# The output projection of a gated MLP as seven block products instead of eight, in a two-block transformer kernel on one NeuronCore

## Chip, core and metric

The kernel runs on one core of one Trainium2 chip, as one program. A time is the device time of one execution in microseconds (us); the time of a kernel is the median of its executions. A profile is of one execution, taken by the hardware profiler. The engines are named as the profile names them: PE (matrix multiply) with PEld (its weight loads), DVE (vector), ACT (scalar), POOL (GpSimd) and SP, which here only issues transfers (DMAs). All loads and stores that this text speaks of go through SP's one queue, in the order of the program.

## What is computed

Two layers over 1024 tokens of width 1024, batch 1, float32. The first block is a dilated attention beside a linear recurrence, whose outputs are merged; the second is a gated MLP, and then a sliding-window attention that shares k and v computed from the MLP's result. The change is in the MLP's last line:

```python
def gmlp_mixer(h, w_in, ln_g, ln_b, w_s, b_s, w_out):
    u, v, z = jnp.split(h @ w_in, 3, axis=-1)          # 3 x (1024 x 2048)
    u = jax.nn.gelu(u)
    v = layer_norm(jax.nn.gelu(v), ln_g, ln_b)
    ...                                                # s: a causal mix of v in chunks of 128 tokens
    y = u * s * jax.nn.silu(z)                         # 1024 x 2048
    return y @ w_out                                   # 2048 x 1024: the output projection

h = h + rms_norm_2(y, a_post_g[i])                     # y is the mixer's result here
kv_in = rms_norm_2(h, kv_norm_g)
k_shared, v_shared = kv_in @ w_k, kv_in @ w_v
```

## The kernel before

A float32 product is made of three matmuls of rounded halves (hi times hi, hi times lo, lo times hi), each of 128 rows by 512 columns over 128 inputs. So each operand tile of 128x512 is first split: ACT writes the hi part (`whi`, `y_hi`) and DVE subtracts it from the raw tile (`wlo`, `y_lo`). Matmuls write to banks of PSUM named `pb`, `pd` and `psP`; the same names serve many stages.

The order on every engine is the order in which the Python program issues instructions; nothing reorders them. The matmul loops call `tick()` every four matmuls. A tick counts down delayed stores (`store`, issued on SP some ticks after their data was requested), tries one step of weight loading and splitting (`w_step`: loads `L209`, splits `L285`/`L286`), and steps the lanes, which are Python generators whose `yield n` means "go on n ticks later". What lanes issue is thus laid beside the matmuls.

In order of time the parts that matter here are these. `phase1a` (to about 1150 us) is the dilated attention with its groups, merged per head pair in `lane_m` (POOL's `Og` and `Wb` lines); `phase2` (to 1337 us) the up-projections of both branches and the first output projection. `phase3` computes v (to 1553 us), then z and u in 16 passes of 128 columns each (to about 1870 us). A pass calls `seven`, which forms two 128x1024 results from seven products over half of the inputs instead of eight, with sums of the inputs made before, and differences of the weight blocks made by POOL (`L228`). Within a pass, c1, c5 and c2 are partial results; POOL adds u = c2 + c5 (`L421`) and c5 = c2 + c5 (`L424`), and DVE adds the PSUM banks (`L405`). Then `mixed` multiplies u, s and silu(z) to y (`L2207`, `L2211`, with POOL's `L2205`), and y goes to DRAM, tiles of 128x512 of the buffers Y for the two halves of the tokens.

The output projection is `out_proj("a_out", 16, ...)`, called `run(0)` and `run(1)` for the two halves of the tokens, from about 1874 us to 2057 us. Each half makes two column blocks of 512, for each of which it runs 16 k tiles by 4 token tiles by 3 matmuls: 192 matmuls (`L1843`), 768 in all. `stream` brings y back from DRAM (16 loads of 512 KB, `L1950`) and splits it (`L1710`, `L1711`). The result is read from PSUM by ACT (`Square` with a row sum, `L1850`) and by DVE (times the norm's gain, `L1851`). After a half, `norm` runs in `lane_n`: a chain of 11 small DVE instructions for the root mean square, the update of x (`xr`, `L1905`), ACT's squares (`L1910`), a second chain, the scaling (`L1923`), and then transposes on PE with copies by ACT and DVE (`L502`, `L503`), which are the operands `Ahi` and `Alo` of the next stage. That stage, from 2057 us on, forms v, k and q (`w_v`, `w_k`), again by halves of the tokens; its first two products for half 0 run while `norm` of the second half is still going on.

## Time and profile before

| what | value |
|---|---|
| time, median of 3 runs | 2487.09 us (2485.14 to 2487.64) |
| time of the profiled execution | 2485.88 us |
| its span, first to last instruction | 2484.1 us |
| mean granted clock of PE | 0.992 |
| PE busy | 2425.1 us, 98% |
| DVE / ACT / POOL busy | 56% / 41% / 29% |
| mean DMA traffic | 103 GB/s |
| z/u passes | 1553 to 1870 us |
| output projection | about 1874 to 2057 us |

The span is what the engines' instructions cover; the 1.8 us by which the execution is longer lie around it. The granted clock is the share of TensorE's full speed that the chip allowed.

### The profile page before, as it was taken

Reading aid. Unit: us, or ns where it says so; the run is one execution under the profiler, and the core shown is the slowest. Engines: PE = TensorE matmul, PEld = TensorE weight load, DVE = VectorE, ACT = ScalarE, POOL = GpSimd, SP = SyncE. Lnnn points to the kernel's source line nnn. Section 1 sums busy time; section 2 is a strip of 40 time slices with the busy share of each in tenths; the row PEclk is TensorE's granted clock in tenths of the full one; section 3 lists DMA queues with packets and bytes.
Section 4 is the critical chain, followed back from the end, with each engine's and each line's share of the span. In section 5 each row is a group of like instructions: output and inputs, shape, how many; then the busy total and the mean of one; then the engine's idle time right before and its main releaser. Section 6 shows DMA issues by size and latency. Waiting matters only on the chain.

```text
span 2484.1 us, 39818 instructions
## 1 busy us (share of the span) xinstructions
PE 2425.1 (98%) x14987; PEld 1917.3 (77%) x14987; DVE 1392.9 (56%) x3235; ACT 1021.4 (41%) x2515; POOL 714.7 (29%) x975
## 2 busy tenths in 40 slices
PE   8999999999999999999999999999999999999998
PEld 6788777777777777777788778888887887777777
DVE  6765345545454345566747347555556546556545
ACT  4433232223232256564244223444454434566632
POOL 3443044433544000222500244454450003201000
PEclk8999999999999999999999999999999999999999
DMA  5334321211122233466733232333335643100133
GB/s 145 102 107 132 69 68 42 58 43 52 48 56 68 80 93 118 128 212 195 238 143 139 86 110 85 102 102 88 95 102 208 217 131 108 41 19 26 32 117 132
DMA packets 271412, 256.94 MB, mean 103 GB/s; under 512 B 26251, under 2 KB 206539, under 8 KB 271220
## 3 DMA queue, kind: packets, MB, share of 16 engines
q1 hardware_dynamic: 271220, 254.40, 33.4%
q8 instruction: 118, 1.93, 0.3%
q14 instruction: 74, 0.61, 0.1%
HBM read 194.29 MB, written 60.06 MB: 102 GB/s over the span
## 4 chain that ended last, share of the span: by engine, by line
PE 83%; DVE 7%; ACT 4%; DMA 3%; issue 2%; SPq 0%; POOL 0%; DVEq 0%; ACTq 0%; POOLq 0%
PE pd L349 38%; PE pd L391 8%; PE psP L391 7%; PE pb L1843 7%; PE pd L1843 7%; PE psO L1157 2%; PE pb L1122 2%; PE pb L1056 2%; DVE wlo L286 1%; DMA vg<-Vd 1%; ACT P L1086 1%; PE pb L2193 1%; PE pb L349 1%; PE pb L743 1%; PE pb L925 1%
## 5 line engine op out<-in xcount | busy, mean ns | idle before, releaser
L349 PE MATMUL pd<-Ahi,wlo 128*128 128x512 f32 x1232 | 495.1, 402 | 4.0 <-DVE wlo L286 3.9
L349 PE MATMUL pd<-Ahi,whi 128*128 128x512 f32 x1232 | 496.2, 403 | 1.7 <-ACT whi L285 1.2
L349 PE MATMUL pd<-Alo,whi 128*128 128x512 f32 x1232 | 495.4, 402 | 0.3 <-DVE Alo L503 0.3
L286 DVE TENSOR_TENSOR wlo<-wraw,whi 128x512 fp32r<-128x512 f32 x356 | 267.4, 788 | 130.7 <-ACT whi L285 127.4
L349 PEld LDWEIGHTS pd<-Ahi,whi 128*128 128x128 f32 x1232 | 233.5, 190 | 54.4 <-issue 2.4
L349 PEld LDWEIGHTS pd<-Ahi,wlo 128*128 128x128 f32 x1232 | 233.4, 189 | 53.7 <-DVE wlo L286 5.4
L349 PEld LDWEIGHTS pd<-Alo,whi 128*128 128x128 f32 x1232 | 233.6, 190 | 52.8 <-issue 4.6
L285 ACT ACTIVATE whi<-wraw 128x512 fp32r<-128x512 f32 x356 | 203.3, 621 | 34.2 <-DMA wraw<-in_b_w_out_dram 12.4
L1711 DVE TENSOR_TENSOR wlo<-wraw,whi 128x512 fp32r<-128x512 f32 x144 | 121.0, 851 | 84.8 <-ACT whi L1710 84.8
L1086 ACT ACTIVATE P<-P,ST 128x192 f32<-128x192 f32 (+2 forms) x320 | 130.6, 409 | 57.6 <-DVE ST L1074 51.0
L1710 ACT ACTIVATE whi<-wraw 128x512 fp32r<-128x512 f32 x144 | 89.5, 623 | 91.4 <-POOL wraw L228 88.8
L349 PE MATMUL pd<-wlo,Ahi 128*128 128x512 f32 x256 | 101.6, 397 | 5.4 <-DVE wlo L286 5.4
L799 POOL TENSOR_TENSOR X<-UC,X 128x60 f32<-128x60 f32 (+24 forms) x248 | 78.1, 315 | 82.5 <-DVE UC L792 64.1
L349 PE MATMUL pd<-whi,Ahi 128*128 128x512 f32 x256 | 100.9, 394 | 0.1
L349 PE MATMUL pd<-whi,Alo 128*128 128x512 f32 x256 | 100.6, 393 | 0.0
L228 POOL TENSOR_TENSOR wraw<-wraw 128x512 f32<-128x512 f32 x48 | 63.0, 1313 | 98.7 <-DVE wlo L1711 90.1
L801 POOL TENSOR_TENSOR X<-X 128x60 f32<-128x60 f32 (+24 forms) x248 | 79.6, 321 | 19.4
L1157 PEld LDWEIGHTS psO<-PT,V 128*64 128x64 f32 x1040 | 55.5, 137 | 35.7 <-issue 17.7
L1157 PE MATMUL psO<-PT,V 128*64 128x128 f32 x1040 | 76.1, 283 | 6.0 <-DVE PT L1138 3.6
L278 POOL TENSOR_TENSOR wraw<-wraw,bpg 128x512 f32<-128x512 f32 x32 | 35.0, 1123 | 154.9 <-DMA wraw<-in_b_w_in_dram 142.9
L1122 PE MATMUL pb<-K,P 128*128 128x128 f32 (+1 forms) x388 | 62.5, 289 | 14.1 <-DVE P L1106 14.1
L1588 ACT ACTIVATE far<-pd 128x512 f32<-128x512 f32 x36 | 33.0, 918 | 101.9 <-PE pd L349 88.5
(434 smaller groups left out, 5398.7 us busy)
## 6 DMA issues: line engine op xcount, KB each, us to landing
wraw<-in_w_in_dram SPq DMA_DIRECT2D x82, 512.0 KB
wraw<-in_a_w_in_dram SPq DMA_DIRECT2D x48, 512.0 KB
wraw<-in_a_w_out_dram SPq DMA_DIRECT2D x32, 512.0 KB
QD<-far SPq DMA_DIRECT2D x36, 256.0 KB
gate<-GT SPq DMA_DIRECT2D x32, 256.0 KB
wraw<-in_w_out_dram SPq DMA_DIRECT2D x16, 512.0 KB
X<-xr SPq DMA_DIRECT2D x16, 512.0 KB
Vd<-v SPq DMA_DIRECT2D x32, 256.0 KB
```

Of the source, the lines that this page charges most:

```text
L285: nc.scalar.activation(out=his[j], in_=t[:, s], func=AF.Copy)
L286: nc.vector.tensor_tensor(out=los[j], in0=t[:, s], in1=his[j].bitcast(F32), op=ALU.subtract)
L349: nc.tensor.matmul(ps, lhsT=a, rhs=b, start=(n == 0), stop=(n == last))
L391: nc.tensor.matmul(ps, lhsT=a, rhs=b, start=(n == 0), stop=(n == 11))
L799: nc.gpsimd.tensor_tensor(out=tv, in0=U[:, j:j + 1, 0:j].to_broadcast([128, w, j]), in1=X[:, b0:8, j:j + 1].to_broadcast([128, w, j]), op= ...
L801: nc.gpsimd.tensor_tensor(out=X[:, b0:8, 0:j], in0=X[:, b0:8, 0:j], in1=tv, op=ALU.add)
L1086: nc.scalar.activation(out=it["P"][j][:, c], in_=Sx[j][:, c], func=AF.Exp, scale=-1.0, bias=ST[:, 0, n:n + 1], accum_out=ST[:, 1, n:n + 1])
L1122: tr = lambda x, m=128: nc.tensor.transpose(ps[0:m, 128 * x:128 * x + 128], Pt[:, 128 * x:128 * x + m], self.ident)
L1157: nc.tensor.matmul(O(h).rearrange("p (s x) -> p s x", s=2), lhsT=V[:, b - 1 + t, c:c + 64], rhs=rhs, start=t == tiles[0], stop=t == 1)
L1710: nc.scalar.activation(out=hi, in_=src, func=AF.Copy)
L1711: nc.vector.tensor_tensor(out=lo, in0=src, in1=hi.bitcast(F32), op=ALU.subtract)
L1843: nc.tensor.matmul(ps[j], lhsT=a, rhs=b, start=(k == 0 and n == 0), stop=(k == KT - 1 and n == 2))
```

## The change

With the inputs of the projection split in two halves of 1024 (A11, A12 for the first half of the tokens, A21, A22 for the second) and its weights in four blocks B11 to B22, the four result blocks are made from seven products of blocks, as `seven` does it for z and u: S1 = A21 + A22, S2 = S1 - A11, S3 = A11 - A21, S4 = A12 - S2 on the left, T1 = B12 - B11, T2 = B22 - T1, T3 = B22 - B12, T4 = B21 - T2 on the right, with the products A11 B11, S1 T1, S2 T2, A12 B21, S4 B22, S3 T3 and A22 T4 in this order.

Three places change. The z/u passes run in the order 0, 8, 1, 9, ..., so that both column halves of y are at hand, and a new lane (`sums`) makes the S tiles on POOL: one subtraction in a pass with a column tile under 8, three operations in the other, 32 of 128x512 in all; 56 tiles of 256 KB go to DRAM (`Y7`) in place of 32. Beside the dilated attention a new lane (`out_weights`) loads the four weight blocks tile by tile (32 loads of 256 KB), makes the T tiles on POOL (32 of 128x512) and stores them (32 stores of 256 KB, `TW`). And `out_proj` returns `run7` for `a_out`: seven products of 8 k tiles by 4 token tiles by 3 matmuls, 96 each, with the partial results joined by ACT, DVE and POOL; `norm(0)` starts behind product 4, `norm(1)` behind product 6.

```diff
-        by_half = lambda name, n: [dt(f"{name}{h}", [n, 128, 512]) for h in range(2)]
-        self.Y = by_half("Y", 16)
+        self.Y7 = [dt(f"Y7_{n}", [8, 128, 512]) for n in range(7)]
+        self.TW = [dt(f"TW{n}", [8, 128, 512]) for n in range(4)]
...
+        self.order_z = [8 * h + c for c in range(8) for h in range(2)]
+        fm("a_zu", a_in, [c for ct in self.order_z for c in (4096 + 128 * ct, 128 * ct)], kind="s")
+        self.first["a_out"] = len(pc)
+        v = km(I["a_w_out_2"][0])
+        T_ = lambda n: self.TW[n].rearrange("k p f -> p k f")
+        for b in (v[:, 0:8, 0:512], T_(0), T_(1), v[:, 8:16, 0:512], v[:, 8:16, 512:1024], T_(2), T_(3)):
+            for k in range(0, 8, 2):
+                pc.append((b[:, k:k + 2, :], "k", None))
...
+    def out_weights(self):
+        nc = self.nc
+        W = self.I["a_w_out_2"][0]
+        def load(r, c, k):
+            t = self.s2("tw")
+            nc.sync.dma_start(t, W[1024 * r + 128 * k:1024 * r + 128 * k + 128, 512 * c:512 * c + 512])
+            return t
+        def minus(x, y, to, n, k):
+            nc.gpsimd.tensor_tensor(out=to, in0=x, in1=y, op=ALU.subtract)
+            if n is not None:
+                self.store(self.TW[n][k], to, 4)
+        for k in range(8):
+            b11, b12, b22 = load(0, 0, k), load(0, 1, k), load(1, 1, k)
+            yield 10
+            minus(b12, b11, b11, 0, k)
+            yield 2
+            minus(b22, b12, b12, 2, k)
+            b21 = load(1, 0, k)
+            yield 2
+            minus(b22, b11, b22, 1, k)
+            yield 6
+            minus(b21, b22, b21, 3, k)
+            yield 5
     def phase1a(self):
         self.att_setup()
...
+        def run7(lanes, sums):
+            self.lanes = lanes + [sums]
+            self.w_lim = 12
+            og, x = ({}, {}), ({}, {})
...
+            def out(c, half, j, t, eng):
+                jk = self.s2("junk")
+                nc.scalar.activation(out=jk, in_=t, func=AF.Square, accum_out=ss[half][:, c, j:j + 1])
+                eng.tensor_tensor(out=t, in0=t, in1=gpost[:, 512 * c:512 * c + 512], op=ALU.mult)
+                og[half][c, j] = t
+            def plus(ps, t, to):
+                nc.vector.tensor_tensor(out=to, in0=ps, in1=t, op=add)
+                return to
+            def evac(n, j, ps):
+                if n < 2:
+                    t = (c1, c5)[n][j] = self.s2("og")
+                    nc.scalar.copy(out=t, in_=ps)
+                elif n == 2:
+                    c2[j] = plus(ps, c1[j], self.s2("og"))
+                elif n == 3:
+                    out(0, 0, j, plus(ps, c1[j], c1[j]), nc.gpsimd)
+                    u[j] = self.s2("og")
+                    nc.gpsimd.tensor_tensor(out=u[j], in0=c2[j], in1=c5[j], op=add)
+                elif n == 4:
+                    out(1, 0, j, plus(ps, u[j], u[j]), nc.vector)
+                elif n == 5:
+                    plus(ps, c2[j], c2[j])
+                    nc.gpsimd.tensor_tensor(out=c5[j], in0=c2[j], in1=c5[j], op=add)
+                    out(1, 1, j, c5[j], nc.gpsimd)
+                else:
+                    out(0, 1, j, plus(ps, c2[j], c2[j]), nc.vector)
+            i0 = self.first[name]
+            for n in range(7):
+                ps = [self.bank() for _ in range(3)] + [self.pd.tile([128, 512], F32, tag="pd", name="pd")]
+                if n == 1:
+                    self.drain(sums)
+                    self.flush()
+                    self.lanes = lanes
+                self.jit_limit = 4 * n + 8 if n else 6
+                if n in (4, 6):
+                    load_x(n // 6)
+                for kp in range(4):
+                    w = self.w_get(i0 + 4 * n + kp)
+                    for j in range(4):
+                        for k in (2 * kp, 2 * kp + 1):
+                            ah, al = [t[:, 128 * j:128 * j + 128] for t in act(k, n)]
+                            wh, wl = w(k % 2)
+                            for m, (a, b) in enumerate(((ah, wh), (ah, wl), (al, wh))):
+                                nc.tensor.matmul(ps[j], lhsT=a, rhs=b, start=(k == 0 and m == 0), stop=(k == 7 and m == 2))
+                        if kp == 3:
+                            evac(n, j, ps[j])
+                    self.w_free(i0 + 4 * n + kp)
+                if n == 4:
+                    self.lane_n.add(norm(0, og[0], x[0], ss[0], 18, 2))
+            self.drain(self.lane_n)
+            self.w_lim = 1000
+            self.lane_n.add(norm(1, og[1], x[1], ss[1]))
+            self.act_f, self.act_t = self.act_views(Ahi, Alo)
+            self.act_tiles = Ahi, Alo
...
+        return run7 if name == "a_out" else run
...
+        def sums(ct):
+            c = ct % 8
+            def do(x, y, op, n, to=None):
+                t = self.s2("ysum") if to is None else to
+                nc.gpsimd.tensor_tensor(out=t, in0=x, in1=y, op=op)
+                self.store(self.Y7[n][c], t)
+                return t
+            yield 4
+            if ct < 8:
+                do(ys[ct, 0], ys[ct, 1], ALU.subtract, 5)
+                yield 2
+                return
+            s1 = do(ys[c, 1], ys[ct, 1], ALU.add, 1, ys[c, 1])
+            yield 3
+            s2 = do(s1, ys.pop((c, 0)), ALU.subtract, 2)
+            yield 3
+            do(ys[ct, 0], s2, ALU.subtract, 4)
+            yield 3
...
-                self.store(self.Y[half][ct], y)
+                ys[ct, half] = y
+                n = {(0, 0): 0, (1, 0): 3, (1, 1): 6}.get((ct // 8, half))
+                if n is not None:
+                    self.store(self.Y7[n][ct % 8], y)
+                if half:
+                    lane_y.add(sums(ct))
...
-                if n == 1 and ct == 15:
-                    actY = self.stream(self.Y, 16, 4, 2)
-                    self.out2 = self.out_proj("a_out", 16, "a_post_g_2", self.X1, self.X2, "plain", actY)
-                if n == 2 and ct:
+                if n == 1 and n_ == 15:
+                    actY = self.stream(self.Y7, 8, 4, 2)
+                    self.out2 = self.out_proj("a_out", 8, "a_post_g_2", self.X1, self.X2, "plain", actY)
+                if n == 2 and n_:
...
-        self.w_lim = 1000
-        self.flush()
-        self.jit_limit = 8
-        self.out2(0, [self.lane_n])
-        self.jit_limit = 16
-        self.out2(1, [self.lane_n])
+            self.seven(i0 + 2 * n_, out, hook)
```

Three places of the order follow. The names are the program's tiles, a line number is that of the kernel whose row it is.

The first is POOL in the z/u stage, one pass before the change: the weight differences of a pass are `L228`, the sums of its partial results `L421` and `L424`, and `L2205` a sum for y's gate.

```order
L228 TENSOR_TENSOR wraw<-wraw 128x512
L228 TENSOR_TENSOR wT_15033<-wraw 128x512
L421 TENSOR_TENSOR c<-c 128x512
L228 TENSOR_TENSOR wraw<-wraw 128x512
L228 TENSOR_TENSOR wraw<-wraw,wT_15033 128x512
L424 TENSOR_TENSOR c<-c 128x512
L2205 TENSOR_TENSOR c<-c,tz 128x512 x2
```

After the change, the end of one pass and the next up to its `L421` (`L2289` is the new lane, `L2346` stands where `L2205` stood):

```order
L2289 TENSOR_TENSOR ysum<-y 128x512
L421 TENSOR_TENSOR c<-c 128x512
L228 TENSOR_TENSOR wraw<-wraw 128x512
L228 TENSOR_TENSOR wraw<-wraw,wT_16288 128x512
L424 TENSOR_TENSOR c<-c 128x512
L2346 TENSOR_TENSOR c<-c,tz 128x512 x2
L228 TENSOR_TENSOR wraw<-wraw 128x512
L228 TENSOR_TENSOR wT_16473<-wraw 128x512
L2289 TENSOR_TENSOR y<-y 128x512
L2289 TENSOR_TENSOR ysum<-y 128x512
L2289 TENSOR_TENSOR ysum<-y,ysum 128x512
L421 TENSOR_TENSOR c<-c 128x512
```

One new operation stands ahead of `L421` in a pass with a column tile under 8, and three in the next; nothing else moved within a pass.

The second is SP at the end of the z/u passes, before the change: `Y_87` and `Y_88` are the two halves' y in DRAM, `yraw` the tile that y is loaded back into, `wraw` a piece of weights.

```order
L172 DMA Y_87<-y 128x512
L172 DMA Y_88<-y 128x512
L1950 DMA yraw<-Y_87 128x2x512 x2
L1409 DMA row<-in_a_post_g_dram 128x1024
L209 DMA wraw<-in_a_w_out_dram 128x2x512 x2
L163 DMA Y_87<-y 128x512
L163 DMA Y_88<-y 128x512
L1950 DMA yraw<-Y_87 128x2x512 x4
L209 DMA wraw<-in_a_w_out_dram 128x2x512
```

After the change (`Y_0_87` to `Y_6_93` are the left operands of products 0 to 6 in DRAM, `TW_94` the right one of product 1):

```order
L172 DMA Y_0_87<-y 128x512
L2068 DMA yraw<-Y_0_87 128x2x512 x2
L1420 DMA row<-in_a_post_g_dram 128x1024
L172 DMA Y_5_92<-ysum 128x512
L209 DMA wraw<-in_a_w_out_dram 128x2x512
L209 DMA wraw<-TW_94 128x2x512
L2068 DMA yraw<-Y_0_87 128x2x512 x2
L172 DMA Y_3_90<-y 128x512
L172 DMA Y_6_93<-y 128x512
L2068 DMA yraw<-Y_1_88 128x2x512 x2
L172 DMA Y_1_88<-y 128x512
L209 DMA wraw<-TW_94 128x2x512
```

Before, the last two stores of y stand ahead of six of the first half's eight loads (the rows behind `L163`); now the four loads of product 0 stand ahead of the last two stores of y, and the loads of product 1 are spread between and behind them and the stores of the last sums.

The third is DVE at the end of the projection, before the change: `wlo` is a weight split, `og` the result read from PSUM, and the rows from `ost` on are the chain of `norm(1)`.

```order
L1851 TENSOR_TENSOR og<-pd,row 128x512 x2
L286 TENSOR_TENSOR wlo<-wraw,whi 128x512 x16
L1851 TENSOR_TENSOR og<-pb,row 128x512 x2
L1851 TENSOR_TENSOR og<-pd,row 128x512 x2
L1898 TENSOR_TENSOR ost<-oss 128x4
L470 TENSOR_SCALAR ms<-ost 128x4
```

After the change (`L1998` adds PSUM to a partial result, `L1994` multiplies it by the gain, `L503` are the last transposes' copies of `norm(0)`):

```order
L1998 TENSOR_TENSOR og<-pb,og 128x512
L1994 TENSOR_TENSOR og<-og,row 128x512
L286 TENSOR_TENSOR wlo<-wraw,whi 128x512
L503 TENSOR_TENSOR Alo<-psT,Ahi 128x4x128
L1998 TENSOR_TENSOR og<-pb,og 128x512
L1994 TENSOR_TENSOR og<-og,row 128x512
L1998 TENSOR_TENSOR og<-pb,og 128x512
L1994 TENSOR_TENSOR og<-og,row 128x512
L503 TENSOR_TENSOR Alo<-psT,Ahi 128x4x128
L1998 TENSOR_TENSOR og<-pd,og 128x512
L1994 TENSOR_TENSOR og<-og,row 128x512
L1939 TENSOR_TENSOR ost<-oss 128x4
```

Eight instructions on the last four banks stand where four stood, the copies and weight splits of the following stage among them.

## Rows read from the trace of the kernel before

**Rows 1.** The page, part 1: busy time, share of the span, instructions.

```profile
PE 2425.1 (98%) x14987; PEld 1917.3 (77%) x14987; DVE 1392.9 (56%) x3235; ACT 1021.4 (41%) x2515; POOL 714.7 (29%) x975
```

**Rows 2.** Windows: stretch, length, busy (instructions) PE, PEld, DVE, ACT, POOL; clock; DMA share, GB/s.

```profile
1553.00:1870.00 317.00, 315.55 (x1498) 259.87 (x1497) 179.11 (x267) 152.78 (x320) 157.04 (x115) 1.00 0.35 102
1870.00:1890.00 20.00, 17.97 (x75) 14.26 (x74) 13.10 (x19) 7.18 (x14) 4.26 (x3) 0.95 0.51 185
1890.00:2057.00 167.00, 166.86 (x748) 137.72 (x748) 83.43 (x150) 66.34 (x141) 12.25 (x18) 1.00 0.52 174
2057.00:2085.00 28.00, 24.47 (x111) 19.84 (x110) 24.63 (x51) 14.41 (x35) 6.87 (x7) 1.00 0.44 138
```

**Rows 3.** The chain that ended last, 1866 to 2100 us: start, duration, what.

```profile
1882.79 4.00 DMA yraw<-Y
1887.56 4.68 PE pb L1843 x12
1892.24 2.72 PE pd L1843 x12
...
2053.84 2.73 PE pd L1843 x12
```

**Rows 4.** PE's waits in 1870:1892, in 2057:2085 and in 1090:1200.

```profile
PE pb L1843 <- ACT y_hi L1710: 2.0, 1, 2.0
...
PE pd L349 <- DVE wlo L286: 3.5, 1, 3.5
...
PE psO L1157 <- DVE PT L1138: 3.6, 2, 2.7
PE pd L349 <- DVE m L1736: 3.5, 2, 1.9
```

**Rows 5.** The waits of SP's queue, 1553 to 1890 us: total, times, longest.

```profile
SPq L163 <- DVE y L2211: 13.0, 2, 12.0
```

**Rows 6.** Groups of instructions, 1553 to 1870 us, POOL.

```profile
L2205 POOL TENSOR_TENSOR c<-c,tz 128x512 f32<-128x512 f32 x30 | 38.8, 1292 | 53.1 <-DVE tz L2218 50.2 <-ACT c L2220 2.9
...
L424 POOL TENSOR_TENSOR c<-c 128x512 f32<-128x512 f32 x14 | 24.5, 1751 | 0.0
```

**Rows 7.** Timeline of POOL 1833 to 1857 us, then of DVE 1845 to 1857 us.

```profile
1846.04 1.29 POOL L228 TENSOR_TENSOR wT<-wraw 128x512 f32<-128x512 f32 x1
1848.62 1.60 POOL L421 TENSOR_TENSOR c<-c 128x512 f32<-128x512 f32 x1 [1.29 <-DVE c L405]
...
1846.66 1.22 DVE L1711 TENSOR_TENSOR wlo<-wraw,whi 128x512 fp32r<-128x512 f32 x1 [2.07 <-ACT whi L1710]
...
1853.64 0.69 DVE L405 TENSOR_TENSOR c<-psP,c 128x512 f32<-128x512 f32 x1
```

**Rows 8.** Timeline of DVE, 2052 to 2078 us.

```profile
2057.32 0.69 DVE L1851 TENSOR_TENSOR og<-pd,row 128x512 f32<-128x512 f32 x1 [0.67 <-ACT junk L1850]
2057.93 0.44 DVE L1898 TENSOR_TENSOR ost<-oss 128x4 f32<-128x4 f32 x1
...
2061.38 5.39 DVE L1905 SCALAR_TENSOR_TENSOR xr<-og,or,xr 128x512 f32<-128x512 f32 x8
2067.20 0.69 DVE L286 TENSOR_TENSOR wlo<-wraw,whi 128x512 fp32r<-128x512 f32 x1 [0.43 <-ACT whi L285]
...
2070.12 0.99 DVE L1916 TENSOR_TENSOR ost<-osv 128x4 f32<-128x4 f32 x1
...
2075.01 1.68 DVE L1923 TENSOR_SCALAR og<-xr,or 128x512 f32<-128x512 f32 x4
2076.60 1.90 DVE L286 TENSOR_TENSOR wlo<-wraw,whi 128x512 fp32r<-128x512 f32 x3
```

**Rows 9.** Groups of instructions of ACT, 1890 to 2085 us.

```profile
L1850 ACT ACTIVATE junk<-pb 128x512 f32<-128x512 f32 x8 | 4.8, 598 | 45.4 <-PE pb L1843 45.1
```

**Rows 10.** Windows in the last merge of the dilated attention, columns as in Rows 2.

```profile
1180.00:1200.00 20.00, 16.48 (x72) 13.02 (x72) 19.60 (x16) 3.03 (x6) 14.42 (x5) 1.00 1.05 342
```

**Rows 11.** The waits of POOL, 800 to 1200 us: total, times, longest.

```profile
POOL Og L1288 <- DMA Wb<-WD: 94.5, 4, 30.8
```

More of the change, by code (lines that the diff above doesn't have):

```diff
@@ L1196, in att_begin, with att_tw @@
         yield 1
+    def att_tw(self):
+        self.lane_t.add(self.out_weights())
+        yield 1
     def att_unit(self, u):
@@ L1626, in phase1a @@
         self.lane_a.add(self.att_begin())
-        self.lanes = self.rw_lanes() + [self.lane_a, self.lane_m]
+        self.lane_t = Lane(2)
+        self.lane_a.add(self.att_tw())
+        self.lanes = self.rw_lanes() + [self.lane_a, self.lane_m, self.lane_t]
         act = self.act_f
@@ L1892, in last, with norm @@
                 nc.sync.dma_start(xdst[128 * tt:128 * tt + 128, s], x[:, s])
-        def norm(half, og, x, ss):
+        def norm(half, og, x, ss, first=12, gap=3):
             yield 2
@@ L1942, in stream @@
         KP = KT // 2
+        NP = len(src) * KP
         raw, hl, big = {}, {}, {}
@@ L1974, in jit @@
             st["wait"] -= 1
-            if st["wait"] <= 0 and st["split"] < min(self.jit_limit, 2 * KP):
+            if st["wait"] <= 0 and st["split"] < min(self.jit_limit, NP):
                 split()
@@ L2197, in phase3 @@
         self.w_lim, self.raw_lim, self.n_prod = 16, 4, 0
-        lane_v.add(v_load(0))
-        for ct in range(16):
+        lane_v.add(v_load(0, 0))
+        lane_y = Lane(2)
+        self.lanes.append(lane_y)
+        ys = {}
+        for n_, ct in enumerate(self.order_z):
             sp, tz, u = {}, {}, {}
```

48 lines of the change are left out of this document (27 added, 21 removed).

## Prediction

> **What bounds the kernel now.** I read the page's first part, then the windows by stage, then the chain that ended last and PE's waits where a window showed PE below full. PE is the bound: it is busy 98% of the span [rows 1], and in the two stages that the change rebuilds it has almost no idle time, 315.55 of 317 us in the z/u passes and 166.86 of 167 us in the projection, at a granted clock of 1.00 [rows 2]. In the projection the chain is PE alone, in steps of 12 matmuls that take 2.72 us [rows 3], or 0.2267 us for one. So matmuls that go away are worth their time, if nothing else becomes the end of a wait. Idle time of PE stands at the edges. Before the projection PE waits 2.0 us for `y_hi` [rows 4], which waits for a load of 4.00 us that SP could issue only at 1882.79 [rows 3]: SP stood 12.0 us in front of the flushed last store of y [rows 5]. Behind that gap the first 12 matmuls take 4.68 us in place of 2.72 [rows 3], with a granted clock of 0.95 in that window [rows 2]: a stretch at the lower level, 1.2 GHz. After the projection PE waits 3.5 us for a `wlo` [rows 4] that stands on DVE behind the chains of `norm(1)` [rows 8]. And in the last part of the dilated attention PE waits for DVE's `PT` and for the merge's `m` [rows 4], where the DMA engines are busy for the whole of a window, 342 GB/s [rows 10].
>
> **The change part by part.** The sum is made against the profiled execution, 2485.88 us (span 2484.1 and 1.8 around it), which lies 1.2 us under the median of 2487.09.
>
> *Matmuls.* 768 become 672: 96 x 0.2267 = 21.8 us less on PE.
>
> *The start of the projection.* Product 0's loads of y now stand on SP ahead of the last stores of y, and product 1's have all of product 0, 96 x 0.2267 = 21.8 us, as cover. The wait of 2.0 us goes, and with it what followed, 4.68 - 2.72 = 1.96 us. I take 3.7 less. If the loads are late all the same, this is 0.
>
> *The z/u passes.* They run the same matmuls in another order of column tiles, so the cost is POOL's 32 sums and 24 more stores. POOL is busy 157 of 317 us there [rows 2]; one such operation takes 1.29 us alone and up to 1.75 us beside DVE work [rows 6], so 32 add 41 to 56 us in idle time of POOL. What can hurt is their place. The three sums of an odd pass stand between `L228` and `L421` (u = c2 + c5). DVE overwrites c2 at 1853.64 and may do so only when `L421` is done, which was at 1848.62 + 1.60 = 1850.22 [rows 7]: 3.4 us of slack. POOL is idle for 1.29 us ahead of `L421` [rows 7], so three sums of 1.29 us (3.9 us) delay it by 2.6 us, within the slack, and three of 1.75 us (5.2 us) by 4.0 us, 0.6 us past it, eight times. Behind it stand DVE's next split and PSUM adds, and PE only when it needs that bank again. Bounds: 0 and 8 us (some 1 us per odd pass); a DVE split that took 1.22 us beside a POOL operation, against its usual 0.69 [rows 7, 8], is a further reason not to take nothing. I take +1.5, nearer the lower end, since PE stands still there for 1.4 of 317 us in all [rows 2] with POOL's eight operations beside it.
>
> *Beside the dilated attention.* 64 transfers of 256 KB, 16.8 MB, and 32 POOL operations (32 x 1.29 = 41 us). Most lie over stretches with idle POOL and DMA. The last of the eight rounds falls to where the DMA engines are full: its 8 transfers, 2.1 MB at 342 GB/s [rows 10], are 6 us of them. POOL waits there for the merge's loads up to 30.8 us [rows 11]; a difference queued behind such a wait is late, and its store holds SP's queue, where weight loads and the merge's own loads stand. PE waits 3.6 and 3.5 us in that part already [rows 4], so a delay there reaches it. Bounds: 0, and 8 us (the 6 us of DMA, with 2 us for lower clock behind a gap as above). I take +3.
>
> *Inside the projection.* Per product DMA brings 2 MB of y and 2 MB of weights in 21.8 us, 192 GB/s, near the 174 of before [rows 2] and far under the 342 of rows 10: no stall. DVE carries more. Product 4's banks end 6 matmuls (1.36 us) apart, but each of the four costs DVE an add (0.69, as the one of rows 7), then ACT's square (0.60 [rows 9], and the read of its sum), then DVE's multiply (another 0.69), some 2.1 us in a row, because the multiply waits for the square in DVE's queue. The fourth ends some 5 us after product 4's last matmul, at 0. Behind it stand two weight splits and two splits of y (4 x 0.6), the chain (2057.93 to 2061.38, 3.45 us), eight `xr` (5.39 us [rows 8]) with two splits of y among them, and then the split of product 5's last weight piece: 5 + 2.4 + 3.5 + 5.4 + 1.2 + 0.7, about 18 us, where PE comes to that piece at 16.3 (three quarters of 21.8): 2 us late. After two more splits of y the second chain (2070.12 to 2075.01, 4.9 us) and the scaling (1.68) [rows 8], two of y and one of weights put the first split of product 6 at 28, against 21.8 and the 2 so far: 4 more. But the chain's price is that of the tail, where its 128x4 add took 0.99 us in place of 0.44 [rows 8]; undisturbed it is some 2 us less. Bounds: 0, if the splits are taken earlier than I reckon, and 8 (2 + 4, and a stretch at the lower clock). I take +3, the middle.
>
> *The tail.* Before, the last PSUM read ended at 2058.0 and the chain of `norm(1)` began [rows 8], 1.5 us after the last matmul (2053.84 + 2.73 = 2056.57 [rows 3]). Now the last four banks are add, square, multiply, 2.1 us each, so the chain begins some 6 us after it, 5 later. Part of that is given back: the `wlo` that ended the wait needs the same DVE queue, and DVE was the one in time by 3.5 us too little [rows 4]. Without cover the whole 5 us are added; with the last two splits ahead of the chain nothing is. Of these I take +4, near the upper end, since DVE is busy 24.63 of 28 us there [rows 2] and has no room to catch up.
>
> The sum: -21.8 - 3.7 + 1.5 + 3 + 3 + 4 = -14.0, so 2485.88 - 14.0 = 2471.9; and 1.2 more for the median: 2473.
>
> On the z/u passes a rule can be weighed against the trace. The Trainium skill, "SBUF — State Buffer", section "Who interferes with whom", has GpSimd share a pair of ports with DVE's second one, as an exclusive lock. The 1.22 us split of rows 7 agrees with it. By that rule an odd pass, of some 21 us, has 11 POOL operations of 1.29 (14.2) and some 11 DVE operations with two SBUF inputs of 0.6 (6.6), 20.8 us in all by this estimate, and so could just be full; that would make the rival below likelier than the rows alone do.
>
> **Rivals.** *All small waits are hidden* (chance 0.15). The added DVE and POOL work finds room, as the whole of POOL's did in the z/u passes so far; the boundary and the 96 matmuls are all that counts, and of the other terms at most 6.5 stay. Then -25.5 to -19, 2460 to 2468 with a us or so of the tail's wait gone as well. For it: DVE is busy 83.43 of 167 us in the projection [rows 2]. Against: its work is not spread, but comes in two bursts.
>
> *DVE's bursts cost all that the matmuls give* (0.13). Each of the joins 4, 5, 6 and the tail costs 5 to 6 us, with a stretch at 1.2 GHz behind each (about 2 us of it, by rows 3): 20 to 25 us in all in place of the 11.5 of my sum, 2482 to 2487, and up to 2492 with the z/u passes at their bound. For it: the 3.5 us wait of rows 4 behind exactly such a burst. Against: weights are split ahead, so a burst of 8 us need not show.
>
> *The z/u passes become slower* (0.07). The place is POOL in front of `L421`. For the kernel to be slower by over 5 us, 19 us beyond my sum must be lost, 2.4 us in each of the eight odd passes: the sums must delay `L421` by 3.4 + 2.4 + the slack of the bank's next use, that is take 2.4 us each in place of 1.29 to 1.75. Then 2492 to 2505. For it: POOL's and DVE's prices rise when they overlap [rows 6, 7]. Against: PE's near freedom from waits there with eight POOL operations a pass [rows 2].
>
> *The change does not take matmuls away* is excluded: 96 rows fewer stand on PE.
>
> **How the numbers follow.** My own case has 0.65, from 2466 to 2481: 2472.9 less 7 and plus 8 for the costs between their bounds. The range from 2460 to 2486 takes in nearly all of the hidden case and the lower part of the no-change case, and leaves out less than 2 in 10. What a measurement of this kernel can tell from no change is about 0.2%, 5 us, 2482 to 2492. Faster: 0.65 + 0.15, less a little of my own case's upper end, 0.79; same 0.14; slower 0.07.
>
> **What would show it.** The projection should last 672 x 0.2267 = 152 us plus its waits, 155 to 162 in all, with no wait on `y_hi` at its start; a few us of waits on `wlo` at the third quarter of product 5, at the start of product 6 and behind the last product, each before a `wlo` behind an `xr` or a chain on DVE. In the z/u stage `L421` should start 2.6 to 4 us later in odd passes and PE's waits stay under 8 us in total. If the stage takes more than 325 us, or if the attention with its merges ends more than 8 us later than before, the prediction is wrong in that term; if PE waits for `yraw` or `wraw` within the projection, the DMA estimate is.

## The result and the profile after

The changed kernel takes 2507.94 us (median of 4 runs, 2507.57 to 2509.84) where the kernel before takes 2486.11 us (4 runs): a ratio of 1.0088, with an interval of 1.0072 to 1.0104. Forecast were 2473 and a range of 2460 to 2486. The profiled execution has a span of 2505.9 us, 21.8 more than before, though PE is busy 6.7 us less (the page's first part):

```profile
PE 2418.4 (97%) x14891; PEld 1904.7 (76%) x14891; DVE 1448.6 (58%) x3263; ACT 1033.9 (41%) x2539; POOL 832.8 (33%) x1055
```

So PE is idle for 28.5 us more (21.8 + 6.7). By the price of 0.2267 us the 96 matmuls that went should have made it busy 21.8 us less; by this estimate the others took 15.1 us longer, at a mean granted clock of 0.987 in place of 0.992.

The windows by stage, columns as in [rows 2]: the last merges of the dilated attention, the z/u passes, the start of the projection, the projection, and what follows it.

```profile
1100.00:1215.00 115.00, 98.92 (x578) 76.56 (x578) 73.54 (x155) 38.75 (x112) 43.44 (x25) 0.94 0.76 237
1567.00:1896.00 329.00, 319.74 (x1498) 261.83 (x1497) 198.43 (x265) 152.56 (x319) 203.88 (x144) 0.99 0.38 115
1896.00:1916.00 20.00, 19.25 (x84) 15.28 (x84) 17.89 (x22) 8.04 (x15) 9.54 (x7) 1.00 0.49 160
1916.00:2073.00 157.00, 146.24 (x644) 118.76 (x643) 105.78 (x173) 76.73 (x158) 35.28 (x34) 0.98 0.63 219
2073.00:2108.00 35.00, 27.63 (x114) 21.26 (x113) 28.55 (x58) 17.33 (x41) 9.30 (x8) 0.95 0.35 111
```

The z/u passes take 329 us for the 1498 matmuls that took 317 before, with 9 us of idle PE in place of 1.4. The start of the projection is clean, as forecast, but behind it 11 of 157 us are idle. From its first to its last matmul the projection takes 172.4 us, where 155 to 162 were forecast (182.1 before). PE's waits name the engines, in 1090:1215, 1567:1896 and 1896:2073; the last row is that of the z/u passes before the change:

```profile
PE pd L349 <- DVE m L1777: 7.4, 4, 2.8
PE pb L1032 <- DVE PT L1138: 4.3, 1, 4.3
...
PE pd L391 <- ACT vg L2311: 9.3, 5, 2.4
...
PE psT L499 <- DVE Alo L503: 6.1, 1, 6.1
PE pb L2037 <- DVE wlo L286: 1.6, 4, 0.7
PE pb L2037 <- ACT whi L285: 1.6, 2, 1.3
PE psT L499 <- DVE og L1998: 1.4, 1, 1.4
...
PE pd L391 <- ACT vg L2173: 1.4, 3, 0.6
```

To see where the 21.8 us went I compare the traces by five marks: the last matmul of the recurrence, the first of the first block's output projection, the first of the mix of v, the last of the z/u passes, and the last transposes behind the MLP. The lengths between them, in us; below the two kernels stand those of the experiments that follow, each where it bears on one:

| kernel | attention and merges | projection of the first block, v | z/u passes | MLP's projection and norms |
|---|---|---|---|---|
| before | 373.7 | 301.0 | 326.9 | 222.6 |
| after | 387.5 | 302.3 | 338.8 | 219.0 |
| before, new order of passes | 371.8 | 301.0 | 326.4 | 225.4 |
| after, stores without sums | 386.6 | 301.7 | 328.8 | 217.8 |
| after, sums later | 387.4 | 302.0 | 351.3 | 222.7 |
| after, load of v earlier | 386.5 | 300.9 | 324.6 | 217.6 |
| before, load of v earlier | 373.4 | 300.9 | 324.6 | 220.5 |
| before, lane of the differences | 385.7 | 302.3 | 326.9 | 222.6 |
| after, no subtractions | 383.9 | 301.0 | 337.9 | 219.3 |
| before, empty step | 376.3 | 301.8 | 328.5 | 222.1 |
| after, differences in short rounds | 378.9 | 302.9 | 337.0 | 220.0 |
| after, these started directly | 369.9 | 301.8 | 338.9 | 218.0 |
| after, started directly, old pauses | 372.6 | 302.3 | 338.3 | 219.6 |
| after, differences beside v | 370.4 | 314.0 | 340.7 | 218.8 |
| after, projection, first edit | 389.3 | 300.9 | 337.2 | 214.1 |
| after, projection, two edits | 388.2 | 302.9 | 336.9 | 213.5 |
| after, projection repaired (three edits) | 387.5 | 301.1 | 338.3 | 208.4 |
| all repairs, first version | 372.4 | 302.1 | 324.6 | 208.0 |
| all repairs, second version | 369.2 | 301.9 | 324.7 | 208.2 |

Each row is one execution. Where no edit touches a part, its length still differs from row to row by 2 to 3 us, and the part ahead of the first mark, the same in all of them, takes 870.7 to 876.1 us; so a difference of under 3 us in this table shows nothing by itself. The kernel before was measured beside every run below. It took 2486.0 to 2486.8 us there, but 2489.54 beside four of them (sums later, differences beside v, and the projection's first edit and first two), whose times are therefore also given against that figure.

So 13.8 us were lost beside the attention, 1.3 with v (no more than that scatter), 11.9 in the z/u passes, and the projection with its norms gained 3.6 where the working behind the forecast had 18.5 (21.8 + 3.7 - 3 - 4).

### The profile page after: what moved, and what is told of

Same layout as the page of the kernel before. It is cut to its first block, busy times and chain, and to the rows that moved or that the text cites. A ratio compares the mean times of both kernels' runs of the same rounds, so it can differ in the third digit from the quotient of the medians.

```text
span 2505.9 us, 40000 instructions
## 1 busy us (share of the span) xinstructions
PE 2418.4 (97%) x14891; PEld 1904.7 (76%) x14891; DVE 1448.6 (58%) x3263; ACT 1033.9 (41%) x2539; POOL 832.8 (33%) x1055
## 5 line engine op out<-in xcount | busy, mean ns | idle before, releaser
L286 DVE TENSOR_TENSOR wlo<-wraw,whi 128x512 fp32r<-128x512 f32 x348 | 279.6, 836 | 148.0 <-ACT whi L285 146.9
L1752 DVE TENSOR_TENSOR wlo<-wraw,whi 128x512 fp32r<-128x512 f32 x144 | 133.0, 934 | 81.1 <-ACT whi L1751 81.1
L228 POOL TENSOR_TENSOR wraw<-wraw 128x512 f32<-128x512 f32 x48 | 66.3, 1382 | 98.6 <-DVE wlo L1752 82.8
L2311 ACT ACTIVATE vg<-vg,lnv 128x128 f32<-128x128 f32 x128 | 53.4, 483 | 52.2 <-DMA vg<-Vd 51.7
```

What stands on the lines that cost most here:

```text
L228: nc.gpsimd.tensor_tensor(out=t[name], in0=t[x], in1=t[y], op=ALU.subtract)
L286: nc.vector.tensor_tensor(out=los[j], in0=t[:, s], in1=his[j].bitcast(F32), op=ALU.subtract)
L1752: nc.vector.tensor_tensor(out=lo, in0=src, in1=hi.bitcast(F32), op=ALU.subtract)
```

## Experiments

### The z/u passes: order, stores or sums

Two runs took the change apart there. The first is the kernel before with the new order of passes alone:

```diff
-        fm("a_zu", a_in, [c for ct in range(16) for c in (4096 + 128 * ct, 128 * ct)], kind="s")
+        self.order_z = [8 * h + c for c in range(8) for h in range(2)]
+        fm("a_zu", a_in, [c for ct in self.order_z for c in (4096 + 128 * ct, 128 * ct)], kind="s")
```

> The kernel before with one edit: the z/u passes in the order 0, 8, 1, 9, ... and nothing else. Theory A, the lost time in the z/u stage (12 us: 317 became 329) comes from POOL's sums and what waits behind them: this run is as fast as the kernel before, within 2 us, with a z/u stage of 317. Theory B, the new order itself makes the loads of weights and of v slower: 8 to 12 us slower, z/u stage 325 or more.

It took 2486.9 us, a ratio of 1.000 (0.9989 to 1.001): the order costs nothing. The second is the changed kernel without the sums:

```diff
-                t = self.s2("ysum") if to is None else to
-                nc.gpsimd.tensor_tensor(out=t, in0=x, in1=y, op=op)
-                self.store(self.Y7[n][c], t)
-                return t
+                self.store(self.Y7[n][c], x)
+                return x
```

> The changed kernel without the sums of y on POOL; the stores stay in number, size and place and store y itself, so the sums are left out of the result. Theory A (POOL's sums): the z/u stage returns to 317 to 319 us, 10 to 12 us faster than the changed kernel. Theory C (the 24 more stores in SP's queue and on the DMA engines): it stays at 326 to 329.

2495.6 us, 12.3 less than the changed kernel, and 328.8 us for the stage by the marks, where the kernel before has 326.9 and the changed one 338.8 (the 317 and 329 of the expectation are windows some 10 us shorter): 10 of the 12 us are the sums, 2 the stores. My rival of the prediction had named POOL in front of `L421`, so I moved the sums behind it:

```diff
-            yield 4
+            yield 14
             if ct < 8:
...
             s1 = do(ys[c, 1], ys[ct, 1], ALU.add, 1, ys[c, 1])
-            yield 3
+            yield 5
...
-            yield 3
+            yield 1
             do(ys[ct, 0], s2, ALU.subtract, 4)
-            yield 3
+            yield 1
```

> The changed kernel with the sums of y begun 14 ticks into the next pass in place of 4, so that they stand behind the two sums L421 and the weight differences on POOL. If the place of the sums in POOL's order is the cause (they hold the weight differences, so the next weight load, and the load of v behind it on SP): the z/u stage, 338.8 us from the first product on v to the last z/u matmul, falls to 328 to 331, and the time by 8 to 11 us. If it is POOL's total work or its sharing of ports with DVE: 336 to 339, and no change.

That was a miss by both readings: 2525.67 us, 36.1 above the kernel before beside it, and 351.3 us for the stage. The sums now stood around `L424` and in front of `L2346`, and DVE's waits for POOL's `L2346` rose from 30.1 to 44.3 us. So this run says that a later place is worse, not that the place in front of `L421` is harmless; that is shown below, where the sums stand there and PE waits for nothing. What costs shows in one pass of the changed kernel in which PE waits 2.42 us; timelines of SP, POOL, ACT, DVE and PE:

```profile
1618.50 0.38 SPq L209 DMA_DIRECT2D wraw<-in_a_w_in_dram  x1
...
1619.56 0.43 SPq L209 DMA_DIRECT2D wraw<-in_a_w_in_dram  x1
1620.09 1.03 SPq L2308 DMA_DIRECT2D vg<-Vd  x1
...
1621.73 1.74 POOL L2289 TENSOR_TENSOR ysum<-y 128x512 f32<-128x512 f32 x1
1623.43 1.74 POOL L421 TENSOR_TENSOR c<-c 128x512 f32<-128x512 f32 x1
1625.13 1.29 POOL L228 TENSOR_TENSOR wraw<-wraw 128x512 f32<-128x512 f32 x1
...
1629.52 0.88 ACT L2311 ACTIVATE vg<-vg,lnv 128x128 f32<-128x128 f32 x2 [7.09 <-DMA vg<-Vd]
...
1631.23 0.62 ACT L2363 ACTIVATE tz<-c 128x512 f32<-128x512 f32 x1
1631.75 0.62 ACT L1751 ACTIVATE whi<-wraw 128x512 fp32r<-128x512 f32 x1
...
1631.88 0.69 DVE L2364 SCALAR_TENSOR_TENSOR tz<-tz,c 128x512 f32<-128x512 f32 x1 [7.26 <-ACT tz L2363]
1632.49 0.69 DVE L1752 TENSOR_TENSOR wlo<-wraw,whi 128x512 fp32r<-128x512 f32 x1
1633.10 0.68 DVE L405 TENSOR_TENSOR c<-pd,c 128x512 f32<-128x512 f32 x1
...
1633.92 0.50 PE L391 MATMUL pd<-S1h,whi 128*128 128x512 f32 x1 [2.42 <-ACT vg L2311]
```

Read from the end: PE needs the bank `pd`, which DVE's `L405` empties until 1633.78. That stands in DVE's queue behind `tz`, which waits for ACT; ACT stood 7.09 us in front of `vg`, the load of v for the pass. POOL had long finished `L421`, at 1625.17. The load of v was issued at 1620.09, late in its pass, because it stands on SP behind two weight loads, and the first of these waits for a buffer that DVE's weight split gives free (222.2 us in all over the stage, shown below). That split hangs in turn on ACT's `whi`, which stands behind `vg`, and on POOL's differences, which stand behind the sums: a loop from pass to pass, through four queues. Two runs took the load of v out of it, one on each kernel, by issuing it a quarter of a pass earlier, ahead of both weight loads, with a longer pause before ACT's work on it:

```diff
-                yield 9
+                yield 15 if n_ > 2 else 9
...
+                if n == 5 and 0 < n_ < 14:
+                    while 1 not in sp:
+                        lane_s.step()
+                    lane_v.add(v_load(n_ + 2, self.order_z[n_ + 2]))
...
-            if n_ < 15:
+            if n_ < 2:
                 lane_v.add(v_load(n_ + 1, self.order_z[n_ + 1]))
```

> The changed kernel with one edit in the z/u stage: the load of v for a pass is issued after the sixth product of the pass before the one that issues it now, so on SP ahead of the weight loads that wait for their buffers. Theory V (the load of v stands in SP's queue behind weight loads that wait for splits; POOL's sums make those late, and a late v holds ACT and DVE, which makes the next splits late): the stage, 338.8 us from the first product on v to the last z/u matmul, falls to 326 to 330, and the time by 9 to 12 us. Theory D (DVE and POOL block each other at the SBUF ports, and the load of v is only what the wait is put down to): it stays above 335.

> The kernel before, with the load of v issued earlier as in the first run of this call. If the load of v ended the waits of the z/u stage already before the change, without slack (three passes of 22.1 to 22.4 us in place of 21.5): the stage falls from 326.9 by 1 to 3 us, and all passes take 21.5. If the stage had slack: no change within 1 us.

On the changed kernel: 2491.67 us, 16.3 less, and the stage takes 324.6 us, under the 335 that theory D asks for. Its window has no idle time of PE at all, with all of POOL's sums in it; the second row is DVE's weight splits there:

```profile
1564.00:1878.50 314.50, 314.50 (x1497) 259.91 (x1496) 212.89 (x270) 156.78 (x325) 206.29 (x144) 1.00 0.41 124
...
L1752 DVE TENSOR_TENSOR wlo<-wraw,whi 128x512 fp32r<-128x512 f32 x86 | 78.7, 928 | 42.6 <-ACT whi L1751 42.6
```

On the kernel before: 2480.22 us, ratio 0.9984 (0.997 to 0.9999), 324.6 us for the stage. So the stage had stood without slack before the change, with waits of 0.4 to 0.6 us in three passes; the sums only made the loop slower. ACT's queue showed it: in the kernel before ACT already waited for the load of v 14 times, 48.2 us in all. The first row is that of SP in the changed kernel; the others are ACT's in the kernel before, in the changed one, and in these with the early load:

```profile
SPq L209 <- DVE wlo L1752: 222.2, 21, 22.2
...
ACT vg L2173 <- DMA vg<-Vd: 48.2, 14, 4.9
ACT vg L2311 <- DMA vg<-Vd: 51.7, 14, 7.1
ACT vg L2174 <- DMA vg<-Vd: 4.1, 1, 4.1
ACT vg L2311 <- DMA vg<-Vd: 3.6, 1, 3.6
```

A DVE split takes 928 ns beside POOL's 206 us, 779 before. That agrees with the rule that the prediction weighed (the Trainium skill, "SBUF — State Buffer", "Who interferes with whom"), but PE waits for none of it.

### The attention: transfers, subtractions, or a step

> The kernel before, with the lane that loads the weight blocks, makes the differences and stores them beside the dilated attention; nobody reads them. If the attention's part of the loss (the output of the merge is used first at 1259.5 us, where it was 1246.4) comes from this lane alone: 11 to 14 us slower than before. If it came from elsewhere: within 3 us.

The lane of the differences alone, in the kernel before, cost 18 us: 2504.86 us, ratio 1.0071 (1.0056 to 1.0086), more than the 11 to 14 expected. By the marks 12.0 of them lie beside the attention and 3.3 ahead of the first mark, where the two programs do not differ. Next the changed kernel with the transfers but without POOL's subtractions:

```diff
-            nc.gpsimd.tensor_tensor(out=to, in0=x, in1=y, op=ALU.subtract)
             if n is not None:
```

> The changed kernel without the subtractions of the weight blocks on POOL; all 64 transfers stay, and store the raw blocks, so the differences are left out of the result. Theory S (the transfers in SP's queue delay the weight loads behind them): the merge's output is still used first at 1256 to 1260 us, and the time is within 3 us of the changed kernel. Theory P (POOL's subtractions delay the merge or DVE): it is used at 1247 to 1250, and the time is 9 to 12 us lower.

2508.88 us, no gain, though in its profile the attention is 3.6 us shorter: POOL's work is at most a small part of what costs there. Counted from the first mark, the matmuls up to 1100 us run as early as before; all is lost from there to the end of the merges. Two runs moved the transfers away, one into the stage of v, where the new lane's start is no longer a step of the attention's lane either, one by shorter pauses (5 + 1 + 1 + 4 + 2 = 13 ticks a round in place of 25; the expectation says 12):

> The changed kernel with the lane of the weight differences moved from the dilated attention to the stage of v (from the second of its four column blocks on, with slightly shorter pauses). If the attention's loss is SP's queue filled to the last there: 9 to 13 us less than the changed kernel, the merge's output first used at 1246 to 1249 us and the v stage at most 3 us longer. If the transfers cost wherever they stand: the v stage is longer by 8 to 12 us, and the time stays.

> The changed kernel with shorter pauses in the lane of the weight differences (12 ticks a round in place of 25), so that all 64 transfers are issued before 1100 us. Theory S (in the last merges SP's queue is full, and only the transfers there cost): the merge's output is first used at 1247 to 1250 us, 9 to 12 us earlier. If the transfers cost as much wherever they stand in the attention: it stays at 1256 to 1260.

Beside v they gave most of it back: 2507.27 us, 17.7 above the kernel before beside it in place of 21.8, with the attention 17 us shorter and the stage of v 12 us longer. There PE waits 8.4 us for weight splits (5.2 in the changed kernel) and 4.3 us for a split of the first z/u weights. In short rounds: 2501.92 us, 6 less, and the merge's output is first used at 1249.9 us, as theory S has it, with 5 us of the attention's loss left. For these I looked at what else the new lane's start does: it is a step in the attention's lane, and so moves the attention by a tick against the merge and the matmuls.

```diff
+    def att_tw(self):
+        yield 1
...
         self.lane_a.add(self.att_begin())
+        self.lane_a.add(self.att_tw())
```

> The kernel before with one empty step in the attention's lane, where the changed kernel starts the lane of the weight differences; no transfer and no operation is added, only the attention's steps fall one tick later against the merge's and the matmuls. If that shift by itself puts the merge's DVE work in front of the copies PE waits for: 3 to 6 us slower than before, lost at 1100 to 1140 us. If the transfers are the whole cause: within 2 us of before.

The empty step alone makes the kernel before 7.3 us slower: 2493.52 us, ratio 1.0033 (1.002 to 1.0047). DVE's timeline in that run shows how:

```profile
1123.25 0.69 DVE L286 TENSOR_TENSOR wlo<-wraw,whi 128x512 fp32r<-128x512 f32 x1 [2.46 <-ACT whi L285]
1123.86 0.54 DVE L1269 TENSOR_TENSOR mws<-mw,mnat 16x384 f32<-16x384 f32 x1
...
1126.03 0.55 DVE L1273 TENSOR_TENSOR mw<-mw,mws 16x384 f32<-16x384 f32 x1
1126.51 0.67 DVE L1691 TENSOR_TENSOR or_lo<-oa,or_hi 128x512 fp32r<-128x512 f32 x1
1127.11 0.67 DVE L286 TENSOR_TENSOR wlo<-wraw,whi 128x512 fp32r<-128x512 f32 x1
1127.82 0.29 DVE L1137 COPY PT<-pb 64x128 f32<-64x128 f32 x1
```

The merge's five small instructions (1123.86 to 1126.58) now stand between the weight split and the copies `PT` that PE waits for; in the kernel before they ran at 1112.7 to 1115.4. The waits for `PT` are 3.3 and 4.2 us, 7.5 in all; before they were 5.1 in all, the longest 2.7 [rows 4]. Of the 7.3 us the trace shows 2.6 beside the attention, about the scatter of the table, and 2.4 behind it; 3.4 lie ahead of the first mark, where the two programs do not differ. They are a stretch at the lower clock (1.2 GHz) behind waits of 1.7 and 0.7 us that both traces have, as the windows of the kernel before and of this run show:

```profile
98.00:110.00 12.00, 10.05 (x43) 8.12 (x44) 7.80 (x9) 5.96 (x11) 7.51 (x6) 1.00 0.21 66
98.00:110.00 12.00, 9.54 (x29) 7.30 (x29) 8.37 (x10) 5.35 (x10) 6.88 (x5) 0.72 0.22 66
```

So it is not shown that all of the 7.3 us are the step's. Then the lane was started directly, with short rounds and with the old pauses:

```diff
-        self.lane_a.add(self.att_tw())
+        self.lane_t.add(self.out_weights())
```

> The changed kernel with the shorter pauses and the lane of the weight differences started directly, so that the attention's steps stand as they did before the change. If the 3.5 to 5 us that were left with the shorter pauses come from the shift by a step: the merge's output is first used at 1244 to 1247 us, 4 us earlier than with the shorter pauses alone. If they come from the transfers: at 1249 to 1251 as with these.

> The changed kernel with the lane of the weight differences started directly, its pauses unchanged (25 ticks a round, transfers until about 1185 us). If the one-tick shift of the attention's steps is most of the attention's loss of 13 us: the merge's output is first used at 1246 to 1251 us and 8 to 12 us are gained. If the late transfers in SP's queue are: it stays at 1254 to 1259, and under 5 us are gained.

2492.58 and 2492.26 us, 15 to 16 less than the changed kernel, with 369.9 and 372.6 us for the attention (371.8 to 373.7 in the kernel before and its two runs without lane and step). The pauses no longer matter. But the direct start also begins 80 us earlier, so that the last store is issued at 1068.0 us with the old pauses, in place of 1197.2. So the two runs by themselves do not part the shift from the transfers beside the last merges. The place of the loss does: below, the attention and merges are split at the first matmuls on the recurrence's output (`or_hi`) and on the attention's (`oa_hi`), in us.

| kernel | step | last store | first mark to `or_hi` | `or_hi` to `oa_hi` |
|---|---|---|---|---|
| before | no | none | 282.7 | 47.6 |
| before, empty step | yes | none | 286.2 | 45.0 |
| after | yes | 1197.2 | 288.4 | 53.7 |
| after, differences in short rounds | yes | 1037.5 | 287.6 | 47.3 |
| after, started directly, old pauses | no | 1068.0 | 283.0 | 46.1 |
| after, these started directly | no | 918.8 | 280.5 | 45.8 |

All eight traces without the step have 279.4 to 284.2 in the first part, and those with it 286.2 to 290.8, but for the one without POOL's subtractions (284.2); so the step costs 4 to 6 us there, with the subtractions perhaps a part of the 6. All nine with transfers up to the merges have 52.8 to 56.0 in the second part, and the others 45.0 to 47.7: late transfers cost some 8 us, whether the step is there or not. There PE waits for `m`, 7.4 us in the changed kernel and 1.9 with short rounds; DVE makes `m` from the loads of the gate, which SP issues at 1166.75 us behind three of the new lane's loads (1163.73).

### The projection: which queue

PE's longest wait, 6.1 us in product 6, is put down to `Alo` on DVE, but DVE follows ACT's `Ahi`. ACT's and POOL's timelines in the changed kernel:

```profile
2045.55 0.63 ACT L1993 ACTIVATE junk<-og 128x512 f32<-128x512 f32 x1 [3.39 <-POOL og L2015]
...
2048.91 0.63 ACT L1993 ACTIVATE junk<-og 128x512 f32<-128x512 f32 x1 [2.64 <-POOL og L2015]
...
2052.25 0.63 ACT L1993 ACTIVATE junk<-og 128x512 f32<-128x512 f32 x1 [2.62 <-POOL og L2015]
...
2053.92 1.06 ACT L502 ACTIVATE Ahi<-psT 128x512 fp32r<-128x512 f32 x2
...
2049.71 1.29 POOL L1994 TENSOR_TENSOR og<-og,row 128x512 f32<-128x512 f32 x1 [0.83 <-ACT junk L1993]
2050.96 1.26 POOL L2015 TENSOR_TENSOR og<-og 128x512 f32<-128x512 f32 x1
```

Product 5's sums on POOL wait for the multiplication in front of them, that waits for ACT's square, and the square for the sum: 3.4 us a bank. The copies of the transposes stand in ACT's queue behind the last square, and PE behind them. Three runs, each with the edits of the one before; the third also begins the norm's work at other ticks (the numbers 14 and 1):

```diff
-                    nc.gpsimd.tensor_tensor(out=c5[j], in0=c2[j], in1=c5[j], op=add)
+                    nc.vector.tensor_tensor(out=c5[j], in0=c2[j], in1=c5[j], op=add)
...
-                    out(1, 0, j, plus(ps, u[j], u[j]), nc.vector)
+                    out(1, 0, j, plus(ps, u[j], u[j]), nc.gpsimd)
...
-                    self.lane_n.add(norm(0, og[0], x[0], ss[0], 18, 2))
+                    self.lane_n.add(norm(0, og[0], x[0], ss[0], 14, 1, 3))
```

The last number of the third is the pause between the updates of x, 1 before.

> The changed kernel with product 5's second sum on DVE in place of POOL. If the waits of product 6 (6.1 us for Alo and 1.4 us) come from ACT's squares, which wait one after another for POOL's sum and hold the copies of the transposes behind them in ACT's queue: these 7.5 us go, 2 to 3 us of lower clock behind them too, 7 to 10 us in all. If DVE's load is what counts: no gain, or 2 us slower.

2503.65 us, 4.3 less, or 14.1 above the kernel before beside it in place of 21.8; by the marks the projection is 4.9 us shorter. The wait fell from 6.1 to 2.1 us. What holds the rest I did not follow.

> As the run before it, and product 4's multiplications on POOL in place of DVE, where each waits for ACT's square. If DVE's queue behind them is what the waits of 3.2 us at product 5's last piece and at the start of product 6 come from: 2.5 to 4 us less than the run before it. If the chain and the updates of x alone fill DVE: under 1 us.

2502.66 us, 1 less and within what can be told; the marks give 0.6. DVE's multiplications were not the point.

> The kernel with product 5's second sum on DVE and product 4's multiplications on POOL, and with the first norm's updates of x spread over three ticks each in place of one, its transposes begun as many ticks later. If the 3.2 us of waits at product 5's last pieces come from the burst of updates and squares in DVE's and ACT's queues, and the 2.9 us in product 6 from transposes that meet product 5's sums: 4 to 7 us less than without the spreading. If ACT and DVE simply have too much in these two products: the waits move, and the gain is under 2 us.

2499.79 us, 2.9 less, short of the 4 to 7. By the marks the part is 5.1 us shorter (208.4 for 213.5). The times alone do not show this gain, since against the kernel before beside each run this one stands 13.8 us above, the one before it 13.1.

### All repairs together

> All edits that gained, together: the early load of v, the weight differences started directly and with shorter pauses, product 5's second sum on DVE, product 4's multiplications on POOL, the first norm spread. If the losses are separate and add up: 2507.9 less 16 (v), 10 (differences) and 8 (projection), 2474, 6 us less than the kernel before with the early load of v and 12 less than the kernel before. If they share stalls: 2480 to 2486.

2472.05 us, ratio 0.9943 (0.9928 to 0.9958), 14.2 us less than the kernel before and 8.2 less than that with the early load of v: it beats both.

> As the run before it, with the first norm's transposes two ticks earlier and its updates two ticks apart, so that its last copies stand ahead of product 6's last banks on ACT and DVE. If the wait of 2.7 us for Ahi and Alo at the start of the next stage comes from these copies standing behind product 6's sums: 1 to 3 us less. If the earlier transposes meet product 5's sums again: 1 to 3 us more.

2465.38 us, ratio 0.9925 (0.9909 to 0.9941), 20.9 us less than the kernel before. That it is 6.7 less than the first version is not shown to be the edit's: in the projection and norms, where the edit is, the two take 208.0 and 208.2 us, and the difference lies ahead of the first mark (2.4) and in the attention (3.2), where the programs are the same. The waits for `Ahi` and `Alo` behind the projection did fall, from 3.4 to 0.7 us, but one of 3.7 for `whi` came in their place. The single gains, 16.3 (v), 15.4 (differences) and 8.1 (projection), would give 2468; the losses are nearly separate. The waits of the second version in the projection and behind it:

```profile
PE pd L349 <- ACT whi L285: 3.7, 1, 3.7
PE psT L499 <- DVE Alo L503: 2.3, 1, 2.3
PE pb L2037 <- DVE wlo L286: 2.1, 1, 2.1
PE pd L349 <- DVE wlo L286: 2.0, 1, 2.0
```

So the projection and its norms take 208.2 us in place of 222.6 and gain 14.4 of the 25.5 that the matmuls and the start are worth; these waits and the lower clock behind them (0.98 over those 208 us) are among what is missing.

## Why the prediction was wrong

The 96 matmuls were worth their time and the start of the projection came out as worked out: no wait on `y_hi` (0.7 us on `y_lo`), no lower clock there, 19.25 of 20 us busy. That term of 25.5 us stands. The four costs were +11.5 in the sum and are some 47 in the run (21.8 + 25.5).

*The z/u passes, +1.5 with bounds of 0 and 8, were 11.9.* The step that failed is "nearer the lower end, since PE stands still there for 1.4 of 317 us in all", from which I took slack. A PE without waits says nothing of the slack of those it waits for. The load of v had none: ACT waited for it in 14 passes before the change, 48.2 us, and issued earlier it gained 2.3 us in that stage on the kernel before and 14.2 on the changed one. The rival on these passes was right that they would slow down and wrong in its place, `L421`.

*Beside the attention, +3 with bounds of 0 and 8, was 13.8.* Late transfers in the last merges were named, and priced by their bytes (6 us) and the wait behind POOL; this mechanism was right and mis-sized: it is some 8 us, where +3 was taken for all of it. POOL's subtractions, which were to make the stores late, cost at most 3.6 us in one trace and nothing in the time. What I left out is the step: that the new lane's start shifts the attention's lane by a tick costs some 4 us by itself.

*Inside the projection and behind it, +7, was 21.9 (25.5 less the 3.6 gained).* I followed DVE's queue from product 4 on and expected its waits at product 5's last piece and the start of product 6: in the trace PE waits 2.9 us there, forecast 3. The sum has no term for product 5's sums and multiplications on POOL, and I did not ask which queue waits for POOL: ACT's, with the transposes' copies in it. That is 6.1 + 1.4 us and the lower clock behind (0.98 over 157 us). In the tail the idle time is 7.4 us where 3.5 stood; forecast were 4 more. That number came out by luck: the chain of `norm(1)` does begin some 6 us later than before, counted from the last matmul, but the wait for `wlo` behind it is 3.4 us as before, and the rest are waits for copies and a split on ACT and DVE (`Ahi` 1.4, `Alo` 0.7, `whi` 1.9), which the prediction did not have.

With the repairs the kernel takes 2465 to 2472 us, near the forecast of 2473, and no repair brings back a matmul. This does not bear the forecast out: one repair, the early load of v, makes the kernel before faster too. Against that kernel the change, repaired, gains 8 to 15 us.

## What to carry to other kernels

When an engine in a static order shows no waits, look one step back, at what its releasers wait for and how long before they are needed they arrive; a load that another engine waits for in nearly every pass, like that of v here, has no slack, and what is added in its loop of queues can come out as a wait of the engine that showed none. When work goes to an idle engine, list which in-order queues wait for its results, not only whether the engine has room. And start a new lane so that the steps of the old ones stay where they were: an empty step cost some 4 us at the merges here.

## What I had not expected of the hardware

The lower clock follows short waits here: behind the 2.42 us wait at 1631.5 matmuls are spaced by 0.31 to 0.42 us in place of 0.23, and the window of the z/u passes has a granted clock of 0.99 (1.00 before), so that 7.9 us more of waits go with 11.9 us more of time. In the merges it is 0.94 over 115 us. A wait of 3.5 us at 2073 before the change had no such stretch behind it, and the waits of 1.7 and 0.7 us near 100 us had one in one execution and none in another; what decides this the runs do not show.
